# Ordering a hybrid decoder layer's instructions on the scheduler's timeline model instead of its plain one

## The chip, the cores and the metric

One core of a Trainium2 chip runs the kernel. The metric is the device time of one execution in microseconds (us); lower is better. The core's engines are TensorE (PE in the rows, with its weight loads as PEld), VectorE (DVE), ScalarE (ACT), GpSimd (POOL) and the queue of SyncE (SP), which issues every transfer of this kernel. Each of them executes its own list of instructions, one after the other, and waits on semaphores for the others. Which instruction stands where in these five lists is what this document is about.

## What is computed

The reference is one decoder layer on 1024 tokens of width 1024 in float32. Cut to what matters:

```
h = rms_norm(x, norm_mix); proj = h @ w_in            # q, k/v of three branches, gates, hq, hf, hi, hg
o_nsa  = gated sum of compressed, selected and window attention  (8 heads of 64, blocks of 128 queries)
o_hgrn = chunked gated linear recurrence, 4 heads of 128, then rms_norm and a silu gate
x = x + concat(o_nsa, o_hgrn) @ w_out
h = rms_norm(x, norm_ffn); gate, up = split(h @ w_gate_up)   # D_FF = 2816
x = x + (silu(gate) * up) @ w_down
```

## The kernel before

**Split products.** Large products are made of three matmuls each (`mm3`, lines 117 to 119), on a high and a low part of both operands. `split` (lines 110 and 111, with a gain 113 and 114) makes the parts: ScalarE writes the high part, VectorE subtracts it from the source for the low part. So nearly every block of weights passes ScalarE and then VectorE before TensorE can use it. The large projections also use a scheme with seven block products in place of eight, whose sums and differences are made on VectorE and GpSimd.

**The stages**, with the time at which each runs in the profile before: 

- Start (0 to 105 us): seven products of `product4` (called in lines 400 to 410) for two of the input projection's column groups. `acts5` to `acts7` and `acts3` build sums of the activations (lines 334, 349, 362, 381), `weights5` to `weights4` differences of the weights on GpSimd, `x_in` scales the input on GpSimd (line 288), `x_stats` squares the tokens on ScalarE (line 273), and `done1` to `done7` take the results out of PSUM. Products run one after the other on TensorE.
- Recurrence heads (about 105 to 280 us): `head` and `hgrn_head`. A head has seven levels, each with four small float32 matmuls (line 472, which the profile shows as eight), some VectorE work on them (lines 477 to 483), and then the next level. The projection of the next head (`dim_tile`, lines 117 to 119 on `hT_h`, `whi`) has no such chain and fills TensorE between the levels.
- Keys and values (about 280 to 410 us), then attention (410 to 750 us): a loop over units (query block, group, branch) with `score` (lines 918 to 929), `values` (940 to 945) and `prep` (854 to 892). The output projection and, near the end, first pieces of the feed-forward part are placed among the units by hand-set constants (`FILL`, `EXTRA`, `EARLY`, `NFIRST` and others).
- Change-over (750 to 800 us): `operand` (lines 803 to 807) transposes and splits the normalised activations, with sums on GpSimd (1066 to 1068). The last token block's norm is a chain of small VectorE instructions (`rsqrt`, lines 124 to 130) that ends in line 822.
- Gate and up projections (800 to about 1200 us): `gate_up_b` and its helpers, 22 rounds of seven products. Products to be used later go to DRAM (`act_store`, line 1120).
- Down projection (to the end): seven calls of `chain`. Weights come in pages of 512 KB into `rpage`, a ring of three buffers (line 1202); stored products come back in loads of up to 1 MB (line 1184); four 1 MB loads of the residual (`x_load`, line 1208) go to `res`. The third chain's weights (`weights5`, line 1256) are differences of two pages, made on GpSimd.

**What sets the order.** The kernel is written with a tile framework. Python code lists all instructions once, in the order in which it is written; the framework knows what each reads and writes and which buffer it needs. When the `TileContext` of lines 1355 and 1356 closes, its scheduler plays the program through on a model of the machine. Whenever an engine of the model is free, it takes, among the instructions whose inputs and buffers are ready in the model, the one that was written first. So an instruction overtakes one written earlier only where the earlier one is not ready in the model at that moment. The resulting lists are fixed when the program is built: on the chip each engine keeps to its list, and waits where the chip is not as far as the model was. In the program before, 1782 of 7092 instructions on TensorE and 819 of 1967 on VectorE stand ahead of one that was written earlier.

The model before is the framework's plain one: it gives an instruction a duration and an engine a time at which it is free.

## Time and profile before

| | us |
|---|---|
| median of 3 runs | 1424.68 (1423.24 to 1426.06) |
| time of the profiled execution | 1428.78 |
| its span, first to last instruction | 1426.9 |
| TensorE busy | 1371.6 (96%) |
| VectorE busy | 1096.2 (77%) |
| ScalarE busy | 617.7 (43%) |
| GpSimd busy | 444.7 (31%) |

Busy time is the time in which an engine had an instruction under way, so 1426.9 less 1371.6 is what TensorE stood still. The mean granted clock of TensorE was 0.99 of full speed. The profiled execution's time is 1.88 us more than its span.

### The profile page before, as it was taken

The page shows a single profiled execution, that of the slowest core. Times are in us where ns is not written, and L with a number is a line of the kernel's source. Part 1 is how long each engine was busy: PE and PEld are TensorE (multiplying, and loading weights), DVE is VectorE, ACT ScalarE, POOL GpSimd, SP SyncE. Part 2 cuts the span into 40 slices and gives each one's busy share as a digit, 9 for nine tenths or more (in the row PEclk, how much of TensorE's full clock was granted, in tenths as well). Part 3 has the DMA queues.
Part 4 walks back from the last instruction along what each step waited for, and adds up shares of the span by engine and source line. Part 5 has one row for each costly group of instructions (what it writes and reads, how often), then busy time and mean ns, then how long its engine had stood idle before and what let it go on. Part 6 is the DMA issues. An engine that isn't in the chain of part 4 may idle for free.

```text
span 1426.9 us, 20201 instructions
## 1 busy us (share of the span) xinstructions
PE 1371.6 (96%) x7224; PEld 1134.1 (79%) x7224; DVE 1096.2 (77%) x1967; ACT 617.7 (43%) x1203; POOL 444.7 (31%) x377
## 2 busy tenths in 40 slices
PE   8699999999999999999998999999999999999998
PEld 6578888999977777777776788888888888867877
DVE  8985888725778888888867888888888886547874
ACT  5652333333346656666665433333333333424332
POOL 8510111102034433344335432233233320028330
PEclk9899999999999999999999999999999999999999
DMA  7541110121130001000003223333333238976532
GB/s 280 193 118 45 31 30 9 34 71 43 45 134 1 1 1 59 31 16 30 17 15 104 90 94 106 110 97 111 111 111 111 90 110 310 315 244 220 178 115 93
DMA packets 112804, 139.94 MB, mean 98 GB/s; under 512 B 6304, under 2 KB 65856, under 8 KB 112704
## 3 DMA queue, kind: packets, MB, share of 16 engines
q1 hardware_dynamic: 112704, 138.66, 29.6%
q8 instruction: 57, 0.93, 0.3%
q14 instruction: 43, 0.35, 0.1%
HBM read 110.06 MB, written 28.57 MB: 97 GB/s over the span
## 4 chain that ended last, share of the span: by engine, by line
PE 73%; DVE 15%; issue 3%; DMA 3%; POOL 2%; ACT 2%; SPq 0%; ACTq 0%; POOLq 0%; DVEq 0%
PE bank L118 7%; PE bank L119 7%; PE a L118 7%; PE bank L117 7%; PE a L117 7%; PE a L119 7%; PE ps_t L117 4%; PE ps_t L119 4%; PE ps_t L118 4%; DVE wop L111 3%; PE ps_t L940 3%; PE a L944 2%; DMA rpage<-in_w_down_dram 2%; PE a L945 2%; PE ps_t L472 1%
## 5 line engine op out<-in xcount | busy, mean ns | idle before, releaser
L110 ACT ACTIVATE wop<-rpage 128x512 fp32r<-128x512 f32 x180 | 112.2, 626 | 155.7 <-PE bank L119 70.3
L929 POOL TENSOR_SCALAR pbig<-pbig,den,gates 128x640 f32<-128x640 f32 (+7 forms) x128 | 103.4, 811 | 165.7 <-DVE den L928 146.5
L111 DVE TENSOR_TENSOR wop<-rpage,wop 128x512 fp32r<-128x512 f32 x180 | 139.6, 779 | 5.2 <-ACT wop L110 3.1
L943 DVE TENSOR_TENSOR ph<-ps_t,ph 128x512 fp32r<-128x512 f32 x126 | 84.3, 683 | 17.8 <-ACT ph L942 17.0
L942 ACT ACTIVATE ph<-ps_t 128x512 fp32r<-128x512 f32 x126 | 72.6, 595 | 49.0 <-PE ps_t L940 38.4
L118 PE MATMUL bank<-wop 128*128 128x512 f32 x175 | 71.0, 407 | 11.3 <-DVE wop L111 11.3
L940 PE MATMUL ps_t<-ident,pbig 128*128 128x128 f32 x504 | 78.2, 274 | 2.1 <-POOL pbig L929 2.1
L1091 POOL TENSOR_TENSOR tmp<-tmp,rpage 128x512 f32<-128x512 f32 x21 | 31.2, 1486 | 138.6 <-DVE wop L111 130.8
L117 PE MATMUL bank<-wop 128*128 128x512 f32 x175 | 71.2, 408 | 3.2 <-ACT wop L110 2.3
L478 POOL TENSOR_TENSOR kp<-kp,fp 128x256 f32<-128x256 f32 x28 | 20.3, 724 | 162.3 <-PE bank L455 110.7
L119 PE MATMUL bank<-wop 128*128 128x512 f32 x175 | 70.0, 401 | 0.0
L940 PEld LDWEIGHTS ps_t<-ident,pbig 128*128 128x128 f32 x504 | 60.6, 140 | 11.5 <-POOL pbig L929 3.2
L111 DVE TENSOR_TENSOR wop<-act_a,wop 128x512 fp32r<-128x512 f32 x48 | 45.7, 953 | 29.5 <-ACT wop L110 29.4
L117 PE MATMUL a<-whi,hT_h 128*128 128x256 f32 (+1 forms) x232 | 66.6, 287 | 0.0
L118 PE MATMUL a<-wlo,hT_h 128*128 128x256 f32 (+1 forms) x232 | 66.4, 286 | 0.0
L119 PE MATMUL a<-whi,hT_l 128*128 128x256 f32 (+1 forms) x232 | 66.2, 285 | 0.0
L927 ACT ACTIVATE pbig<-ps_s,nm 128x640 f32<-128x640 f32 (+3 forms) x64 | 55.9, 874 | 23.6 <-DVE nm L926 18.2
L1051 POOL TENSOR_TENSOR tmp<-rpage 128x512 f32<-128x512 f32 x20 | 27.2, 1360 | 118.0 <-DMA rpage<-in_w_gate_up_dram 118.0
L110 ACT ACTIVATE wop<-act_a 128x512 fp32r<-128x512 f32 x48 | 30.2, 629 | 72.2 <-PE bank L119 53.2
L926 DVE TENSOR_REDUCE nm<-ps_s 128x1 f32<-128x640 f32 (+3 forms) x64 | 58.1, 914 | 4.2 <-PE ps_s L921 2.8
L944 PE MATMUL a<-ph,kv 128*128 128x512 f32 x132 | 58.6, 444 | 1.8 <-ACT ph L942 1.0
L945 PE MATMUL a<-ph,kv 128*128 128x512 f32 x132 | 56.9, 431 | 2.9 <-DVE ph L943 2.3
(485 smaller groups left out, 4460.1 us busy)
## 6 DMA issues: line engine op xcount, KB each, us to landing
rpage<-in_w_gate_up_dram SPq DMA_DIRECT2D x86, 256.0 KB, 3.1
rpage<-in_w_down_dram SPq DMA_DIRECT2D x40, 512.0 KB, 4.6
act_a<-act_d SPq DMA_DIRECT2D x12, 1024.0 KB, 7.6
act_d<-as SPq DMA_DIRECT2D x33, 256.0 KB, 2.2
rpage<-in_w_in_dram SPq DMA_DIRECT2D x14, 512.0 KB, 5.2
act_e<-act_d SPq DMA_DIRECT2D x6, 1024.0 KB, 7.9
act_d<-tmp SPq DMA_DIRECT2D x22, 256.0 KB, 2.1
act_d<-th SPq DMA_DIRECT2D x22, 256.0 KB, 2.1
```

What stands on the lines that cost most here:

```text
L110: A.activation(hi, src, AF.Copy)
L111: V.tensor_tensor(lo, src, hi.bitcast(F32), op=OP.subtract)
L117: PE.matmul(o, ah, bh, start=first, stop=False, skip_group_check=chained)
L118: PE.matmul(o, ah, bl, start=False, stop=False, skip_group_check=chained)
L119: PE.matmul(o, al, bh, start=False, stop=last, skip_group_check=chained)
L926: V.tensor_reduce(nm, sv, axis=AX.XY, op=OP.max, negate=True)
L929: G.tensor_scalar(pp, pp, den, gates[:, qb, h * 3 + 1 + b:h * 3 + 2 + b], op0=OP.mult, op1=OP.mult)
L940: PE.transpose(pt[:, r * P:(r + 1) * P], wts[r][:, c0:c0 + P], ident)
L942: A.activation(ph[:, 0], pt, AF.Copy)
L943: V.tensor_tensor(ph[:, 1], pt, ph[:, 0].bitcast(F32), op=OP.subtract)
L944: PE.matmul(o, vst[b][:, kb, g, :], ph[:, 0], start=b == 0 and kb == kb0, stop=False)
L945: PE.matmul(o, vst[b][:, kb, g, :], ph[:, 1], start=False, stop=False)
```

## The change

One argument of the `TileContext` is set, so that the scheduler plays the program on the framework's other model, in which each engine, each sequencer and each queue has a timeline of its own (an instruction's decoding, its wait, its execution and the landing of its result are separate pieces). No instruction of the kernel, no operand, no buffer and no constant is edited. What may differ in the program is the place of each instruction in its engine's list, the buffer of a ring that it gets, and the waits that follow from both.

```diff
-    with _tile.TileContext(nc) as tc:
+    with _tile.TileContext(nc, schedule_with_timeline_sim=True) as tc:
         hybrid_layer(tc, *args)
```

## Rows read from the trace of the kernel before

**Rows 1.** The page's first part: busy time, share of the span, instructions.
```profile
PE 1371.6 (96%) x7224; PEld 1134.1 (79%) x7224; DVE 1096.2 (77%) x1967; ACT 617.7 (43%) x1203; POOL 444.7 (31%) x377
```
**Rows 2.** Busy time of each engine by stage: stretch, length, then engines; clock, DMA.
```profile
0.00:100.00 100.00, 80.11 (x310) 62.79 (x311) 91.75 (x136) 58.80 (x100) 57.59 (x44) 0.93 0.59 195
100.00:400.00 300.00, 295.82 (x2050) 269.14 (x2049) 203.43 (x509) 102.30 (x212) 31.62 (x37) 1.00 0.16 46
400.00:700.00 300.00, 289.43 (x1709) 228.42 (x1707) 249.57 (x563) 187.24 (x429) 122.06 (x135) 0.99 0.08 30
700.00:800.00 100.00, 91.00 (x482) 69.93 (x482) 75.51 (x159) 56.54 (x108) 49.67 (x38) 0.98 0.18 53
800.00:1244.00 444.00, 444.00 (x1960) 367.80 (x1959) 357.83 (x466) 147.31 (x241) 116.81 (x80) 1.00 0.41 136
1244.00:1300.00 56.00, 50.13 (x195) 38.08 (x195) 25.78 (x35) 18.57 (x33) 19.31 (x15) 0.94 0.73 246
1300.00:1426.90 126.90, 121.14 (x527) 97.89 (x525) 92.34 (x104) 46.97 (x83) 47.69 (x30) 1.00 0.42 143
```
**Rows 3.** The same view, four stretches of 5 us in the start.
```profile
35.00:40.00 5.00, 1.84 (x6) 0.66 (x4) 5.00 (x8) 3.01 (x6) 5.00 (x5) 1.00 0.00 0
40.00:45.00 5.00, 2.02 (x4) 1.33 (x5) 5.00 (x8) 4.65 (x9) 1.60 (x2) 0.58 0.87 274
55.00:60.00 5.00, 1.09 (x5) 0.56 (x3) 5.00 (x7) 3.60 (x7) 1.97 (x2) 1.00 0.77 245
85.00:90.00 5.00, 1.94 (x6) 1.28 (x6) 5.00 (x10) 3.52 (x6) 0.00 (x0) 0.86 0.00 0
```
**Rows 4.** Timeline of VectorE in the start: start us, us, line, instruction.
```profile
52.33 1.79 DVE L111 TENSOR_TENSOR hT_l<-kv,hT_h 128x512 fp32r<-128x512 f32 x1
54.04 1.79 DVE L362 TENSOR_TENSOR qtok<-kv,sums 128x512 f32<-128x512 f32 x1
55.76 3.57 DVE L381 TENSOR_TENSOR qtok<-kv,sums 128x512 f32<-128x512 f32 x4
59.25 0.68 DVE L111 TENSOR_TENSOR wop<-sums,wop 128x512 fp32r<-128x512 f32 x1
```
**Rows 5.** Timeline of ScalarE just before.
```profile
51.10 0.63 ACT L110 ACTIVATE wop<-sums 128x512 fp32r<-128x512 f32 x1
```
**Rows 6.** Timeline of TensorE there; in brackets the idle time and its releaser.
```profile
60.58 0.50 PE L118 MATMUL bank<-wop 128*128 128x512 f32 x1 [4.50 <-DVE wop L111]
```
**Rows 7.** Line 111, 25 to 66 us: count, least, median and largest ns.
```profile
L111 DVE TENSOR_TENSOR wop<-sums,wop x8: 676/678/1775, 24.2 to 60.5; 128x512 fp32r<-128x512 f32 x8
L111 DVEq EVENT_SEMAPHORE  x6: 21/21/21, 27.2 to 54.9; - x6
```
**Rows 8.** Timelines of VectorE and TensorE in the change-over.
```profile
773.21 0.71 DVE L129 SCALAR_TENSOR_TENSOR rs_t<-rs_t,rs_v 128x1 f32<-128x1 f32 x1
773.44 0.52 PE L803 MATMUL bank<-ident,d 128*128 128x128 f32 x3 [0.72 <-DVE opA L807]
774.44 0.72 DVE L130 SCALAR_TENSOR_TENSOR n_rs<-rs_t,n_rs 128x1 f32<-128x1 f32 x1
775.69 2.31 DVE L822 SCALAR_TENSOR_TENSOR x<-x,n_rs,rpage 128x1024 f32<-128x1024 f32 x1
775.83 0.50 PE L119 MATMUL a<-opA,wop 128*128 128x512 f32 x1 [0.84 <-DVE wop L111]
```
**Rows 9.** The chain of waits in the third chain of the down projection.
```profile
1245.99 6.97 DMA rpage<-in_w_down_dram
1253.13 1.14 POOL tw_p L1256
...
1286.71 2.58 DMA rpage<-in_w_down_dram
```
**Rows 10.** Timeline of the transfer queue before that: issue time, time in the queue.
```profile
1225.17 0.50 SPq L1208 DMA_DIRECT2D res<-x_d  x1
1235.51 0.43 SPq L1208 DMA_DIRECT2D res<-x_d  x1
1240.97 0.94 SPq L1208 DMA_DIRECT2D res<-x_d  x1
```
**Rows 11.** Busy time of each engine over one recurrence head.
```profile
168.00:207.20 39.20, 38.40 (x232) 32.19 (x231) 34.07 (x87) 12.66 (x27) 5.01 (x7) 1.00 0.10 28
```
**Rows 12.** Timeline of TensorE in that head: one level's matmuls, one of the fill's.
```profile
177.01 1.15 PE L472 MATMUL ps_t<-qp,kv 128*128 128x128 f32 x8
177.91 0.48 PE L119 MATMUL a<-hT_h,wlo 128*128 128x512 f32 x1
...
180.13 1.16 PE L472 MATMUL ps_t<-qp,kv 128*128 128x128 f32 x8
```

## The prediction

> **What bounds the kernel now.** I read the page's busy times first, then busy time by stage, and then, where a stage leaves TensorE idle, the timelines of the engines in front of it. TensorE is busy for 1371.6 us [rows 1] of a span of 1426.9. The change neither adds nor takes away a matmul, so the whole stake in the faster direction is the 55.3 us in which TensorE stands still, and what its clock loses after such pauses. By stage [rows 2] that idle time is 19.9 us in the start, 4.2 from 100 to 400, 10.6 in the main part of attention, 9.0 around the change-over, none from 800 to 1244, 5.9 from 1244 to 1300 and 5.8 from there to the end. The sum is 55.3 again.
>
> These stages have different limits. In the start VectorE is full: 5.00 of 5 us in each of the four stretches in which TensorE has its longest pauses, with 1.84, 2.02, 1.09 and 1.94 us of matmuls [rows 3]. One pause can be followed to an instruction. TensorE waits 4.50 us for line 111 [rows 6], which starts at 59.25; its first input left ScalarE at 51.73 (51.10 and 0.63) [rows 5]. Between the two, VectorE ran line 111 for a later product, line 362 and four times line 381 [rows 4]. Line 381 prepares the product at line 409, while TensorE waited for the one at line 407. On the chip these stood in the wrong order, and that is what a closer model could mend. The recurrence heads are near the limit of two engines: of 39.2 us TensorE has 38.40 and VectorE 34.07 [rows 11]. From 800 to 1244 TensorE never stops, and its order there is the written one. Around 1250 the chain of waits is load, GpSimd difference, load: 6.97 us for the first page, 2.58 for the last [rows 9]. The ring of three pages holds the next load back there, not the order alone.
>
> **The change part by part.** It moves instructions and nothing else; I cost it stage by stage, against the profiled execution (span 1426.9, time 1428.78, which is 4.1 us or 0.3% above the median of 1424.68), and carry the difference to the median.
>
> Instructions added: none but waits. A wait of its own on VectorE takes 21 ns [rows 7]; a hundred more on one engine would be 2.1 us if none were covered. Their number may also fall, so I take 0, with 2.1 either way.
>
> Start: if the four line 381 instructions run behind the splits that TensorE waits for, 3.57 us [rows 4] leave a pause of 4.50 [rows 6]. VectorE is full, so the work moved back is in front of something else later; what is late next is the pause from 85 to 90 [rows 3]. I take half, -1.8. The bound below is the idle time of the first three stretches, 3.16 + 2.98 + 3.91 = -10.1. The bound above is the price of bad neighbours. The same instruction took 678 ns in the median and 1775 at most in this stretch [rows 7], when GpSimd was at work [rows 3]; all eight slow would be 8 x 1.10 = +8.8.
>
> The Trainium skill (SBUF — State Buffer, section Who interferes with whom) says that a VectorE instruction with two SBUF inputs and a GpSimd instruction that reads SBUF exclude each other for the whole instruction, whichever comes second. The row's two durations agree with it; by that rule a new order changes durations too, and the start could come out at the +8.8 in place of -1.8.
>
> Heads and keys, 100 to 400: 4.2 us idle in 300, TensorE fed by the fill. I take 0; a gain of 4.2 is the bound below, and the first rival is the bound above.
>
> Attention, 400 to 700: 10.6 us idle in 300 against 4.2 in the 300 before [rows 2]. VectorE (249.57) and ScalarE (187.24) both have room, so the excess of 6.4 is order and latency. I take a quarter, -1.6; the bounds are that excess won or doubled, 6.4 either way.
>
> Change-over, 700 to 800: two small norm instructions (0.71 and 0.72 us) stand between the splits for which TensorE waits 0.72 and 0.84 us [rows 8], and line 822 takes 2.31 us of VectorE right behind. Put after the splits, the two give back -1.4; the bounds are half of the stage's 9.0 idle us, 4.5 either way. The chain they belong to ends the last token block, so it can't be put off far.
>
> Gate and up, 800 to 1244: no idle time, written order, every buffer ring in its turn: 0. What hides a shift of VectorE or of the stores there is TensorE's own 444 us; VectorE has 86 us to spare. If VectorE were given its splits so late that the 86 us were used up, each us beyond them would be one of the total; nothing in the rows points that way.
>
> Down projection: 195 matmuls in 56 us, against 4.41 a us before [rows 2], are 52 too few, or 11.8 us. SyncE's queue issues three 1 MB residual loads (line 1208) just ahead of the slow pages [rows 10]. They are ready whenever the queue has nothing else to do, in either model, so I take 0. If they went elsewhere, half of the 11.8 could be won, and if more large loads came in front, as much lost: 5.9 either way. The queue is one list: what it is moved past counts here, and a page behind one 1 MB load more is late by that load.
>
> Sum: -1.8 - 1.6 - 1.4 = -4.8 us. Span 1422.1, profiled 1424.0, median 1419.9; I forecast **1420**.
>
> **The rivals.** *A critical matmul behind the fill* (slower). The fixed lists hold each level's eight matmuls of a recurrence head between fill matmuls [rows 12]. If the new model takes fill earlier, VectorE gets each level later. The head has 39.2 - 34.07 = 5.1 us of VectorE room, over seven levels 0.73 us each; from that point on TensorE runs out of fill before the chain ends. The levels in the row are 3.1 us apart. Five more fill matmuls in front, at 0.23 (444 us by 1960, [rows 2]), are 1.1 us a level: 7.9 - 5.1 = 2.8 a head, 11.2 over four heads, so 1424.7 + 11.2 = 1435.9. For it: both engines are close to full there and the order before leaves only 0.8 us a head. Against it: a model closer to the chip should see the chain too.
>
> *Neighbours on VectorE and GpSimd* (slower): the start's splits on VectorE meet GpSimd's sums and differences more often, +8.8 [rows 7], 1433.5. It decides where TensorE has no matmul in hand, as in the four stretches of [rows 3]. This is the rule of the Trainium skill (SBUF — State Buffer, Who interferes with whom) that was weighed above.
>
> *The order hardly matters* (no change): pauses are set by the ring of pages, by VectorE's total in the start (91.75 of 100 us, [rows 2]) and by the first load, and TensorE's work is fixed. Then 1424.7. That the new model gives the old lists, so that the change does nothing, belongs here too; with 819 of 1967 VectorE instructions out of written order already, I give that little.
>
> *The whole of the start and of the pages* (faster by more): -10.1 and -5.9, 1408.7.
>
> **How the numbers follow.** About 0.2%, 2.9 us, is what a measurement of this kernel can tell from no change. The forecast gets 0.34 (its own range 1412 to 1422), the large gain 0.12, no change 0.18, the fill rival 0.28 and the neighbours 0.08. So faster 0.46, same 0.18, slower 0.36. Cases of both signs hold most of the chance, so the range is wide. Down it reaches the large gain with the change-over's bound, 1408.7 - 4.5 = 1404. Up it takes the fill rival's 1435.9 and most of the start's bound of 8.8 with it, 1444.
>
> **What would show it.** Right: line 381 behind line 407's splits on VectorE and the pause of 4.5 us near 58 below 2; from 400 to 700 TensorE idle under 9 us; around 775 the norm's small instructions behind the splits; the same matmuls, a busy time of TensorE near 1371 and no idle time from 800 to 1240. Fill rival: heads further apart than 39.2 us, with VectorE waiting for line 472. Neighbours: line 111 in the start at a median near 1.7 us. I am wrong if a stage that I set to 0 moves most, above all the 444 us of the gate and up products or the pages of the down projection.

## The result, and the profile after

The changed kernel takes 1482.01 us (four runs, 1479.4 to 1485.77) for 1425.2 of the kernel before: a ratio of 1.0403, with a 95% interval from 1.0373 to 1.0432. The prediction was 1420, range 1404 to 1444. It had the wrong sign and the wrong size.

The work is the same: the page's busy times, next to [rows 1], show the same instruction counts, TensorE busy 6.4 us longer and VectorE 18.6.

```profile
PE 1378.0 (93%) x7224; PEld 1148.2 (78%) x7224; DVE 1114.8 (75%) x1967; ACT 618.9 (42%) x1203; POOL 455.1 (31%) x377
```

Next, busy time by stage, as [rows 2], but cut at the borders of the work. The borders are read from TensorE's timeline: the first matmul of line 455 (first recurrence head), the last of line 526, the first of line 940 (attention), the last of line 958, the last of line 803, the first of the down projection. In the tables and below, the stages between these borders are called start, heads, keys, attention, change-over, gate/up and down.

```profile
0.00:130.10 130.10, 110.85 (x447) 88.64 (x448) 106.16 (x153) 68.51 (x114) 57.81 (x44) 0.93 0.52 167
130.10:349.00 218.90, 193.53 (x1300) 179.01 (x1300) 142.16 (x334) 62.47 (x122) 28.02 (x28) 0.95 0.10 27
349.00:445.90 96.90, 95.24 (x721) 90.56 (x720) 65.55 (x194) 33.95 (x88) 16.54 (x14) 1.00 0.28 94
445.90:808.30 362.40, 328.15 (x1893) 257.13 (x1893) 278.62 (x623) 216.79 (x481) 138.28 (x148) 1.00 0.05 18
808.30:846.60 38.30, 27.44 (x147) 22.04 (x147) 32.93 (x51) 19.19 (x36) 24.57 (x17) 0.82 0.37 101
846.60:1255.90 409.30, 409.30 (x1800) 338.73 (x1800) 341.62 (x433) 132.84 (x216) 122.41 (x82) 1.00 0.34 111
1255.90:1477.60 221.70, 213.51 (x925) 172.05 (x923) 147.74 (x182) 85.15 (x148) 67.45 (x44) 1.00 0.62 213
```

The heads and the keys of the kernel before, in the same way:

```profile
128.70:281.70 153.00, 149.49 (x968) 129.50 (x967) 131.53 (x331) 52.39 (x105) 20.26 (x28) 1.00 0.10 28
281.70:416.60 134.90, 132.58 (x1040) 128.14 (x1039) 74.27 (x194) 45.03 (x106) 15.60 (x12) 1.00 0.25 81
```

All stages at the same borders in the kernel before, and in the runs that follow (us; each line adds up to the span of the run's profiled execution, 1426.9 before and 1477.6 after):

| run | start | heads | keys | attention | change-over | gate/up | down |
|---|---|---|---|---|---|---|---|
| before | 128.7 | 153.0 | 134.9 | 335.4 | 35.9 | 409.7 | 229.3 |
| after | 130.1 | 218.9 | 96.9 | 362.4 | 38.3 | 409.3 | 221.7 |
| e1_heads_back | 128.8 | 178.2 | 135.4 | 360.6 | 38.7 | 408.7 | 222.2 |
| e2_heads_forth | 129.4 | 209.9 | 102.3 | 335.1 | 36.2 | 408.1 | 225.4 |
| e3_pe_back | 133.7 | 179.8 | 134.6 | 352.7 | 39.3 | 408.9 | 223.9 |
| e4_fill_256 | 130.2 | 213.2 | 96.8 | 361.7 | 38.3 | 409.5 | 223.1 |
| e5_pe_dve_back | 132.2 | 153.1 | 136.0 | 346.7 | 35.6 | 408.3 | 229.1 |
| e6_four_back | 130.4 | 153.1 | 134.9 | 335.5 | 35.9 | 408.1 | 224.1 |
| e7_dve_forth | 140.1 | 179.9 | 134.3 | 356.6 | 40.2 | 408.7 | 227.2 |
| e8_down_forth | 128.4 | 153.0 | 134.9 | 335.5 | 35.9 | 409.7 | 221.9 |
| e9_copy_first | 128.8 | 164.8 | 134.9 | 334.3 | 35.9 | 409.7 | 226.0 |
| e10_fill_first | 128.0 | 166.5 | 134.9 | 336.4 | 35.9 | 408.1 | 226.8 |
| e11_act_forth | 134.3 | 153.2 | 136.0 | 347.2 | 36.2 | 408.4 | 224.9 |
| e12_sum_back | 139.9 | 173.7 | 134.3 | 359.6 | 40.2 | 408.5 | 223.4 |
| e13_fold_first | 130.7 | 153.2 | 134.9 | 335.3 | 35.9 | 408.1 | 227.4 |
| e14_attn_forth | 130.8 | 153.0 | 140.3 | 392.7 | 34.8 | 409.9 | 225.8 |
| e15_end_back | 140.2 | 162.1 | 134.3 | 356.7 | 39.7 | 408.6 | 223.4 |

The heads take 65.9 us more and the keys behind them 38.0 less, because fill (independent projection matmuls) that belonged to the keys' time was done in the heads; together they lose 27.9. Of this, 21.3 is time in which TensorE stands still (27.0 now, 5.8 before, by the rows above). The other 6.7 is longer busy time, with 13 more matmuls in the two stages and a mean granted clock of 0.95 in the heads, 1.00 before. The attention loses 27.0. The down projection shows 7.6 less, the rest moves by 3 at most.

TensorE's waits over the whole program (waiter, what came last; us in total, times, longest) name the places; before, these four were 0.6, 2.3, 2.4 and 3.7 us. The fifth line is VectorE's wait in the heads, 4.1 us before.

```profile
PE bank L526 <- DVE qp L523: 13.2, 2, 6.6
PE a L945 <- DVE ph L943: 11.6, 23, 1.7
PE ps_t L472 <- DVE qp L477: 10.2, 9, 1.5
PE ps_s L918 <- ACT pbig L927: 6.1, 15, 0.7
DVE qp L477 <- PE ps_t L472: 22.0, 13, 3.4
```

TensorE's timeline in the first head, next to [rows 12], shows how a head looks now:

```profile
162.88 1.05 PE L472 MATMUL ps_t<-qp,kv 128*128 128x128 f32 x8
166.73 1.05 PE L472 MATMUL ps_t<-qp,kv 128*128 128x128 f32 x8
168.72 1.13 PE L472 MATMUL ps_t<-qp,kv 128*128 128x128 f32 x8 [0.94 <-DVE qp L477]
171.14 1.13 PE L472 MATMUL ps_t<-qp,kv 128*128 128x128 f32 x8 [1.29 <-DVE qp L477]
...
186.28 1.11 PE L526 MATMUL bank<-ident,qp 128*128 128x128 f32 x4 [6.61 <-DVE qp L523]
```

The early levels stand more than 6 us apart (143.98, 150.14, 156.30, 162.88), full of fill. The last ones are bare, with no fill between them: TensorE waits for VectorE, and then for 6.61 us at the head's end, where VectorE normalises the head and nothing is left to do beside it. The program's own list says the same. These are the fill matmuls behind each group of the chain's matmuls (two of line 455, then the seven levels of line 472; a dash is none):

```
              L455 L455  1   2   3   4   5   6   7   ahead of L526
before, head 1  12   9   4   9   6   5   7   7   -   2 + 34
before, head 2  13   9   4   9   6   5   7   7   -   2 + 34
after,  head 1  25  28  23  23  25  13   -   -   -   -
after,  head 2   -  29  25  24  18   -   -   -   -   -
```

Head 2 has 96 fill matmuls in both. In the old list they are dealt out so that each level has about what VectorE's chain needs, and 34 cover the head's end. In the new list all 96 are gone after the third level. Only the first three heads run bare: the fourth has fill behind every level, the fill of the keys. VectorE's list has changed too. In all 28 levels both masked copies L483 now stand ahead of the sum L480, in none before.

Over the whole program 2900 of 6948 matmuls now stand ahead of one written earlier, 1638 before (the figure of 1782 of 7092 given further up counts all of TensorE's instructions, not its matmuls alone); on VectorE 1045 of 1967, 819 before.

### The profile page after: what moved, and what is told of

Read it like the earlier page. It is cut to its first block, busy times and chain, and to the rows that moved or that the text cites. A ratio compares the mean times of both kernels' runs of the same rounds, so it can differ in the third digit from the quotient of the medians.

```text
span 1477.6 us, 20109 instructions
## 1 busy us (share of the span) xinstructions
PE 1378.0 (93%) x7224; PEld 1148.2 (78%) x7224; DVE 1114.8 (75%) x1967; ACT 618.9 (42%) x1203; POOL 455.1 (31%) x377
## 4 chain that ended last, share of the span: by engine, by line
PE 74%; DVE 14%; DMA 4%; issue 3%; POOL 3%; ACT 2%; SPq 0%; ACTq 0%; POOLq 0%; DVEq 0%
PE a L119 9%; PE a L117 9%; PE a L118 9%; PE bank L118 7%; PE bank L119 7%; PE bank L117 7%; PE ps_t L117 4%; PE ps_t L119 4%; PE ps_t L118 4%; DVE wop L111 2%; DVE nm L926 2%; DMA rpage<-in_w_down_dram 2%; DVE ph L943 2%; PE ps_t L940 2%; PE a L945 2%
## 5 line engine op out<-in xcount | busy, mean ns | idle before, releaser
L111 DVE TENSOR_TENSOR wop<-rpage,wop 128x512 fp32r<-128x512 f32 x180 | 145.9, 813 | 16.4 <-ACT wop L110 14.4
L478 POOL TENSOR_TENSOR kp<-kp,fp 128x256 f32<-128x256 f32 x28 | 28.0, 1001 | 210.8 <-PE bank L455 110.8
L118 PE MATMUL bank<-wop 128*128 128x512 f32 x175 | 70.0, 400 | 5.3 <-DVE wop L111 5.2
L945 PE MATMUL a<-ph,kv 128*128 128x512 f32 x132 | 60.1, 455 | 13.1 <-DVE ph L943 11.6
L119 PE MATMUL bank<-wop 128*128 128x512 f32 x175 | 69.1, 395 | 0.0
L117 PE MATMUL bank<-wop 128*128 128x512 f32 x175 | 64.7, 401 | 1.9 <-ACT wop L110 1.9
L111 DVE TENSOR_TENSOR wop<-tmp,wop 128x512 fp32r<-128x512 f32 x42 | 44.6, 1063 | 18.8 <-ACT wop L110 18.0
```

The costliest lines, as they stand in the source:

```text
L111: V.tensor_tensor(lo, src, hi.bitcast(F32), op=OP.subtract)
L117: PE.matmul(o, ah, bh, start=first, stop=False, skip_group_check=chained)
L118: PE.matmul(o, ah, bl, start=False, stop=False, skip_group_check=chained)
L119: PE.matmul(o, al, bh, start=False, stop=last, skip_group_check=chained)
L945: PE.matmul(o, vst[b][:, kb, g, :], ph[:, 1], start=False, stop=False)
```

## The experiments

**How lists were exchanged.** Both schedulers emit the same instructions in the same five lists (one per engine, and SyncE's transfers), in different order. So one engine's list, or a stretch of it, can be taken from the other program. Each instruction of the list gets an order-only dependency on the one ahead of it; the scheduler then orders only what is left free. So the lists that aren't pinned can change as well, and a run shows the pinned list together with what the scheduler arranges around it.

```diff
+def _pin(nc, tc, engine, text):
...
+    for a, b in zip(seq, seq[1:]):
+        tc.add_manual_dep(own[b], own[a].name, NOSYNC, reason="pin")
...
         hybrid_layer(tc, *args)
+        _pin(nc, tc, PE, ORDER_OF_BEFORE)
```

The long names in capitals stand for lists of instruction numbers, `PE` and the like for engines, `NOSYNC` for the order-only kind of dependency. e6_four_back shows below that the pins themselves cost nothing.

**TensorE's list of the heads, put back into the changed kernel (e1) and taken into the kernel before (e2).**

```diff
+        _pin(nc, tc, PE, HEADS_OF_BEFORE)   # e1, with the timeline
+        _pin(nc, tc, PE, HEADS_OF_AFTER)    # e2, without it
```

> The timeline model schedules everything, but TensorE's list for the four recurrence heads is pinned to the one of the kernel before (1064 matmuls). Theory A (the loss of the heads is TensorE's fill, taken in batches too long for the chain of a head): the heads are 39 us apart again instead of 51 to 58, and the time falls by the 29 us by which the first attention transpose (line 940) was late, to about 1453 (1445 to 1460). Theory B (the loss sits in the lists of the other engines, as in line 478 on GpSimd, whose mean rose from 724 to 1001 ns): the heads stay over 45 us apart and the time over 1470.

> The reverse: the plain model schedules everything, but TensorE's list for the four heads is pinned to that of the changed kernel. Theory A: the heads are 50 to 58 us apart and the time rises by about 29 us, to 1454 (1445 to 1462), though the lists of all other engines come from the plain model. Theory B: the heads stay near 40 us apart and the time within 10 us of 1425.

Measured: e1 1479.57 us, ratio 1.0379 (1.0344 to 1.0413); e2 1452.14, ratio 1.0182 (1.0161 to 1.0203). The second is what the fill theory said, the first is not. TensorE's new list of the heads costs 24.3 us net in the old program (heads +56.9, keys -32.6 in the table), most of the 27.9 of the changed kernel. The plain scheduler arranged the other lists around it: VectorE's heads changed too, but no level has both copies ahead of the sum. The bare levels show the difference: the last two of the first head are 2.08 us apart in e2, as shown here, and 2.42 in the changed kernel's fence (168.72 and 171.14):

```profile
167.98 1.13 PE L472 MATMUL ps_t<-qp,kv 128*128 128x128 f32 x8 [0.94 <-DVE fp L480]
170.06 1.13 PE L472 MATMUL ps_t<-qp,kv 128*128 128x128 f32 x8 [0.94 <-DVE fp L480]
```

But putting the old list back into the new program gives almost nothing back: the heads still take 178.2 us. Something else in the new program holds them then.

**TensorE's whole list put back (e3), and the fill in half-size matmuls (e4).**

```diff
+        _pin(nc, tc, PE, ORDER_OF_BEFORE)   # e3, with the timeline
```
```diff
-            sl = slice(hf * 512, (hf + 1) * 512)
-            for c in range(NK):
-                wh, wl = parts[c]
+            for q in range(2):
+                sl = slice(hf * 512 + q * 256, hf * 512 + (q + 1) * 256)
+                for c in range(NK):
...
```

> The timeline model schedules everything, but TensorE's whole list is that of the kernel before; the other four lists are free to differ. Theory A, carried to attention as well: nearly all of the loss is in TensorE's list, so the time is 1417 to 1430; if the 8 us that the changed kernel wins in the down projection come from the other lists, it is below 1425. Theory B: over 1450.

> The timeline model, and the heads' projections (dim_tile) as matmuls of 256 columns, twice as many and each half as long; no arithmetic is left out. In the changed kernel a batch of 23 to 28 fill matmuls of 512 columns, over 5 us, stands between two levels of a head. Theory A1 (the model hands TensorE a number of instructions ahead, whatever they take): still some 28 a batch, so half the time, 3.3 to 3.6 us, and the heads move closer, under 50 us apart; time 1460 to 1475. Theory A2 (the model reckons a level's work on VectorE as over 5 us long, and fills that time): some 50 a batch, the heads as far apart as in the changed kernel (51 to 58 us), time 1475 to 1490.

Measured: e3 1474.39 us, ratio 1.0331 (1.0312 to 1.035); e4 1474.71, ratio 1.0341 (1.0321 to 1.0362). In e3 TensorE does its matmuls in exactly the old order, and heads (179.8) and attention (352.7) are slow all the same: a list can be late on an engine that isn't the busiest. In e4 the list has 51, 37 and then mostly 28 halves behind a group, where the changed kernel has 25, 28 and 23 wholes. In head 1 that is 264 halves up to the last level, for 137 wholes; they reach further down the levels, but at the head's end none are left again. The batch of 28 and the time are what the first expectation said, but the heads stay 48.5 to 56.9 us apart, nearer to the second. They take 213 us for 219. Smaller pieces don't cure it.

VectorE's list in e3 shows what is late. It isn't the changed kernel's list, as the new model made it around TensorE's old one: 24 of its 28 levels have both copies ahead of the sum. The first fence is one level of a head in the kernel before, the second one in e3 (VectorE's and GpSimd's timelines).

```profile
184.49 0.76 DVE L477 TENSOR_TENSOR qp<-qp,fp 128x256 f32<-128x256 f32 x2
185.16 0.27 DVE L480 TENSOR_TENSOR fp<-fp 128x64 f32<-128x64 f32 x1
185.34 0.76 DVE L483 COPY_PREDICATED kv<-hm,ps_t 128x256 f32<-128x256 uint8 x2
185.57 0.64 POOL L478 TENSOR_TENSOR kp<-kp,fp 128x256 f32<-128x256 f32 x1 [1.29 <-DVE fp L480]
186.00 0.50 DVE L478 TENSOR_TENSOR kp<-kp,fp 128x256 f32<-128x256 f32 x1
```
```profile
197.91 0.75 DVE L483 COPY_PREDICATED kv<-hm,ps_t 128x256 f32<-128x256 uint8 x2
198.57 0.25 DVE L480 TENSOR_TENSOR fp<-fp 128x64 f32<-128x64 f32 x1
198.93 0.43 DVE L478 TENSOR_TENSOR kp<-kp,fp 128x256 f32<-128x256 f32 x1
198.97 0.90 POOL L478 TENSOR_TENSOR kp<-kp,fp 128x256 f32<-128x256 f32 x1 [1.60 <-DVE fp L480]
199.29 1.18 DVE L477 TENSOR_TENSOR qp<-qp,fp 128x256 f32<-128x256 f32 x2
```

Before, the sum L480, on which both halves of L478 wait, goes first, and the two masked copies L483 fill the time in which GpSimd does its half of L478. In e3 the copies go first, and GpSimd's half runs beside L478 and L477 on VectorE: 0.90 us for 0.64, and L477 takes 1.18 us for two instead of 0.76.

**Which engine's list: VectorE's as well put back (e5), then ScalarE's and GpSimd's too (e6), and e3's VectorE list taken forth (e7).**

```diff
+        _pin(nc, tc, PE, ORDER_OF_BEFORE)
+        _pin(nc, tc, DVE, ORDER_OF_BEFORE)   # e5, e6: with the timeline; e7: DVE's list of e3, without it
+        _pin(nc, tc, ACT, ORDER_OF_BEFORE)   # e6
+        _pin(nc, tc, POOL, ORDER_OF_BEFORE)  # e6
```

> The scheduler with the timeline, with TensorE's and VectorE's whole lists taken from the kernel before; ScalarE's, GpSimd's and the queues' lists stay the new ones. Theory B (VectorE's own list carries what was left after TensorE's list was put back: in each level of a head the masked copy L483 now stands ahead of the sum L480, on which the next level waits, and L478 and L477 on VectorE run beside L478 on GpSimd): 1425 to 1436 us, heads 39 to 40 us apart, L477 back from 549 ns to 420 ns in the mean. Theory C (ScalarE's, GpSimd's or the queues' lists carry it): above 1450 us, heads 44 us apart or more.

> The scheduler with the timeline, with the lists of TensorE, VectorE, ScalarE and GpSimd all taken from the kernel before: what is left of the change is SP's queue alone. If the queue's order carries nothing: 1426 us within 3. If the gain of some 6 us that the changed kernel shows in the down projection is the queue's (its fetches issued in another order): 1418 to 1422 us. If the queue carries a loss: above 1432 us.

> The plain scheduler with TensorE's list of before, and VectorE's list of the run e3_pe_back. Theory B (VectorE's list alone makes the loss of e3_pe_back): 1455 to 1475 us, heads 44 to 48 us apart, attention (first to last matmul of L940 to L958) 345 to 355 us for 335 before. Theory C (ScalarE, GpSimd or the queues): below 1435 us.

Measured: e5 1442.59 us, ratio 1.0113 (1.0097 to 1.013); e6 1426.24, ratio 1.0002 (0.9991 to 1.0013); e7 1485.74, ratio 1.0421 (1.0402 to 1.044). e5 brings the heads back to 39.2 us apart and leaves 11 us in the attention and some 4 in the start, so it lies between the two theories: of the loss of e3, VectorE's list carries the heads, and ScalarE's or GpSimd's a part of the rest. e6 is the kernel before again: SyncE's new order is worth nothing either way. e7 is above its 1455 to 1475. TensorE's list is as before, and e3's VectorE list with what follows from it costs as much as the whole change: 27 us in the heads, 21 in the attention, 11 in the start. What follows includes ScalarE's list, which differs from that of before in 258 of 1203 places, 151 of them in the attention, so the 21 us there aren't shown to be VectorE's alone.

**The down projection alone (e8).**

```diff
+        _pin(nc, tc, PE, DOWN_OF_AFTER)   # and DVE, ACT, POOL, SP; without the timeline
```

> The plain scheduler with the lists of all five engines taken from the changed kernel in the down projection alone (the last 924 matmuls, SP's last 100 fetches). If the 6 to 7 us that the changed kernel wins behind the gate and up products are its order there: 1417 to 1421 us, faster than both kernels. If they come from the state that the earlier stages leave (what has been fetched by then): 1424 to 1428 us.

Measured: 1422.12 us (12 runs), ratio 0.9977 (0.9968 to 0.9986), the fastest of all kernels here. That is between the two expectations. The gain is real but half as large as the profiles say: 3.4 us by the medians for 7.4 in the stage (229.3 to 221.9). The stage takes 224.1 us in e6 and 227.4 in e13, with the old order in it on all four compute engines; the profiled execution of the kernel before was a long one (1428.78 us for a median of 1425.2). In e8, ScalarE and GpSimd run their instructions in the same order of lines and tiles as before, so the gain comes from TensorE's or VectorE's order there, with SyncE's or without. In the stage's row of e8 TensorE is idle for 8.8 us, 11.6 before.

```profile
1197.40:1419.30 221.90, 213.08 (x925) 172.15 (x923) 148.39 (x182) 85.27 (x148) 67.44 (x44) 1.00 0.63 213
```

**One place at a time, in the kernel before: the copies ahead of the sum (e9), the fill ahead of the chain (e10), ScalarE's list (e11).** The edits are changes of a list. In e9 `477 477 480 483 483 478` becomes `477 477 483 483 480 478` in all 28 levels. In e10 the fill behind the levels 1 to 7 of the first three heads, `4 9 6 5 7 7 -`, becomes `13 12 13 - - - -` (the 19 behind levels 4 to 6 move; the expectation says 21), and that of the fourth head likewise.

```diff
+        _pin(nc, tc, PE, ORDER_OF_BEFORE)      # e10: FILL_FIRST instead, no other pin
+        _pin(nc, tc, DVE, COPY_FIRST)          # e9
+        _pin(nc, tc, DVE, ORDER_OF_BEFORE)     # e11, POOL too
+        _pin(nc, tc, ACT, ORDER_OF_E5)         # e11
```

> The plain scheduler with TensorE's list of before and VectorE's list of before but for one thing: in each of the 28 levels of the heads the sum L480 stands behind the masked copies L483 that followed it. Theory B (this place alone makes the heads' loss of the runs e3_pe_back and e7_dve_forth): two copies of 0.76 us each level ahead of what the next level waits for, 28 x 0.76 = 21 us, to 27 us with L477 slowed by GpSimd's L478 beside it: 1444 to 1454 us, heads 44 to 46 us apart, attention 335 us. Rival (the fill's work on VectorE between the levels, L546 to L556 and L111, makes it): below 1432 us, heads under 41 us apart.

> The plain scheduler with TensorE's list of before but for one thing: in each head the fill matmuls that stood behind the levels 4 to 7 (21 of 38 in the first three heads, most of them) are spread over levels 1 to 3, in the same order, so that levels 4 to 7 stand bare; no work is moved from one head to another or out of the heads. Theory A (fill costs nothing only while VectorE's chain of the same level runs): the moved fill, 0.23 us each, lengthens the early levels and the bare ones don't get shorter than VectorE's 2.4 us: some 3 to 6 us a head, 12 to 24 in all: 1437 to 1450 us, heads 42 to 45 us apart. Rival (TensorE is busy 97% of the heads, so the order of the same work is worth nothing): 1424 to 1429 us, heads 39 us apart.

> The plain scheduler with the lists of TensorE, VectorE and GpSimd of before, and ScalarE's list of the run e5_pe_dve_back. If ScalarE's order makes the 17 us of that run: 1438 to 1446 us, attention 344 to 350 us for 335 before. If GpSimd's order or the queue's makes it: below 1430 us, attention 335 to 337 us.

Measured: e9 1439.34 us, ratio 1.0101 (1.0081 to 1.012), heads 42 us apart; e10 1438.21, ratio 1.0095 (1.0075 to 1.0116), heads 41.5 to 43.8; e11 1442.39, ratio 1.0117 (1.01 to 1.0133), attention 347.2.

e9 falls between its two expectations. The place costs 11.8 us over 28 levels, 0.42 each and not 0.76 (what covers the rest was not traced); it is a cause, but less than half of VectorE's 27. The groups of the heads show the slowed pair: VectorE's L477 and GpSimd's L478 in e9, 420 and 724 ns in the mean before.

```profile
L477 DVE TENSOR_TENSOR qp<-qp,fp 128x256 f32<-128x256 f32 x56 | 27.1, 524 | 4.6 <-PE ps_t L472 4.0
L478 POOL TENSOR_TENSOR kp<-kp,fp 128x256 f32<-128x256 f32 x28 | 26.2, 937 | 168.1 <-PE bank L455 110.1 <-DVE fp L480 58.0
```

e10 bears the fill theory out: no matmul left its head, only 19 of them (some 4.3 us at 0.23) moved a few levels up, and the first two heads grew by 2.3 and 2.4 us, the third by 4.7, the fourth by 4.0. Of the 13.5 us, 9.2 are idle time of TensorE and 4.3 longer busy time, at a mean granted clock of 0.96 in the heads. VectorE's list wasn't pinned: the fill's L546 and L548 moved up with their matmuls in the first three heads, and no level has both copies ahead of the sum. The bare levels are 2.07 us apart, so the chain alone sets a pace, and TensorE stands still in it:

```profile
190.33 1.13 PE L472 MATMUL ps_t<-qp,kv 128*128 128x128 f32 x8 [1.18 <-DVE qp L477]
192.40 1.13 PE L472 MATMUL ps_t<-qp,kv 128*128 128x128 f32 x8 [0.94 <-DVE fp L480]
```

e11 answers what e5 left: with the lists of TensorE, VectorE and GpSimd as before, ScalarE's list alone gives e5's time and nearly its stages (17 us by the medians, 12 of them in the attention). In the start, TensorE waits 14.5 us for splits of line 110, 7.7 before.

**The rest of VectorE's loss in the heads: the sum put back into e7 (e12), a second thing put back (e15), and the fill's VectorE work one place earlier in the kernel before (e13).**

```diff
-... 477 477 483 483 480 478 ...
+... 477 477 480 483 483 478 ...           (e12: 18 of 28 levels of e7's list)
-... 516 ... 111 ... 552 ... 518 111 521 521 554 523 523
+... 516 ... 518 521 521 523 523 111 552 111 554   (e15: e12's list, end of head 3; head 2's alike; one 111 in head 1's)
-... 478 546 477 ...
+... 546 478 477 ...                       (e13: 12 places of the list of before)
```

> The kernel of e7_dve_forth (TensorE's list of before, VectorE's list as the model of e3_pe_back orders it) with one thing put back: in 18 of the 28 levels, where the copies L483 stand right ahead of the sum L480, the sum goes back in front of them. If the place of the sum costs as much here as in e9_copy_first (12 us for 28 levels): heads 42 to 43 us apart and 1473 to 1480 us. If the places add up to more together (a level delayed in two places misses TensorE's fill as well): heads back to 40 us, 1465 us or below. If the sum's place was no cause here: heads 44 to 48 us apart, 1483 us or more.

> VectorE's list of before but for one thing: the 12 places in the first three heads where a query or gate operation of the fill (L546 or L548, 0.68 us) stands right behind the chain's product L478 are swapped, the fill's operation first. Theory B2 (VectorE's 0.68 us of fill ahead of the chain lengthens a level like the copies do): 4 x 0.4 to 0.68 us a head, 5 to 8 us: 1430 to 1434 us, heads 40.8 to 42 us apart. Rival (the level has room, or the swap is hidden beside GpSimd's half of L478): within 2 us of 1425.5, heads 39.2 us apart.

> The kernel of e12_sum_back with a second thing put back on VectorE: at the end of the first three heads the fill's operations that stand among the head's normalisation ahead of L523 (three weight splits L111 of 1.21 us in the first two heads' ends and one more in the third, the second L552 and L554) go behind L523, where the kernel before has them. If they make TensorE's waits at L526 (10.8 us in e12_sum_back, 0.6 before): those waits under 3 us, heads 43 us apart in the mean, 1466 to 1471 us. If L523 is late for another reason (the head's chain itself ends late): waits at L526 stay over 7 us and the time within 3 us of 1476.7.

Measured: e12 1476.73 us, ratio 1.0357 (1.0332 to 1.0381); e13 1425.29, ratio 0.9996 (0.9987 to 1.0006); e15 1468.71, ratio 1.031 (1.0288 to 1.0333). e13 is a clean miss for its theory: a fill operation of 0.68 us ahead of VectorE's half of L478 costs nothing, in 12 places. Not every operation ahead of the chain counts. e12 wins 6.2 us in the heads (179.9 to 173.7), the size that it should. In e12 the trace shows where to look next, TensorE's waits in the heads:

```profile
PE bank L526 <- DVE qp L523: 10.8, 4, 4.2
PE ps_t L472 <- ACT kv L468: 6.2, 4, 1.6
```

and VectorE's timeline ahead of one of them, where two weight splits of the fill (the second starts at 224.77), L552 and L554 stand among the head's last operations, ahead of L523:

```profile
220.91 1.22 DVE L111 TENSOR_TENSOR wlo<-wraw,whi 128x1024 fp32r<-128x1024 f32 x1 [0.32 <-ACT whi L110]
222.76 0.69 DVE L552 TENSOR_TENSOR fp<-a,kv 128x512 f32<-128x512 f32 x1
224.77 1.21 DVE L111 TENSOR_TENSOR wlo<-wraw,whi 128x1024 fp32r<-128x1024 f32 x1
225.90 0.42 DVE L554 TENSOR_SCALAR kp<-fp 128x512 f32<-128x512 f32 x1
226.24 1.28 DVE L523 TENSOR_TENSOR qp<-qp,gmix 128x512 f32<-128x512 f32 x2
226.97 0.66 PE L526 MATMUL bank<-ident,qp 128*128 128x128 f32 x4 [4.25 <-DVE qp L523]
```

e15 moves nine such operations behind L523, and the heads fall by 11.6 us more, to 162.1, with the wait nearly gone:

```profile
PE bank L526 <- DVE qp L523: 2.3, 4, 0.7
```

So of the 26.9 us that VectorE's list costs in the heads of e7, the sum's place is 6.2, the ends of the heads 11.6; 9.1 are left, of which 6.2 is the wait of L472 for ScalarE above: once a head, at the third level, behind the one place where the list still has the copies (in the first three heads L548 too) ahead of the chain's products. That place wasn't tried by itself. How far this carries over to the changed kernel differs: its own VectorE list has the copies ahead of the sum in every level, but between L516 and L523 it has nothing but the head's own operations, in all four heads. The 11.6 us belong to e3's list; in the changed kernel the head's end waits because the fill is gone.

**TensorE's list in the attention alone (e14).**

```diff
+        _pin(nc, tc, PE, ATTENTION_OF_AFTER)   # without the timeline
```

> The plain scheduler with TensorE's list of the changed kernel in the attention alone (the other engines' lists are the plain scheduler's own). If TensorE's order carries its own part of the attention's 27 us (362 in the changed kernel against 353 with TensorE's list back): attention 343 to 350 us, 1434 to 1441 us. If the attention's loss is only VectorE's and ScalarE's: 334 to 338 us, 1424 to 1428 us.

Measured: 1489.4 us, ratio 1.0441 (1.0416 to 1.0466); the attention takes 392.7 us, far more than in the changed kernel. TensorE's waits there name the place: its new list takes the output projection early, and the pages for it (lines 606, 607) come late.

```profile
PE a L117 <- DVE rpage L606: 17.7, 4, 11.9
PE a L119 <- DVE rpage L607: 10.8, 6, 2.9
```

The other lists aren't those of before either: the plain scheduler arranged them around this one, and VectorE's has 12 of the 16 conversions of line 606 in the first third of the operations of line 943, as the changed kernel has, for 8 before. So this run can't size TensorE's part, nor is it shown why the pages are late. What the exchanges do show is that parts of them don't add up. In heads and keys, TensorE's new heads list in the old program costs 24, e3's VectorE list beside TensorE's old one 26, and the changed kernel with all its own lists 28.

## Why the prediction was wrong

- **Heads and keys.** This is the step that failed. It was set to 0 with the fill rival as its upper bound of 11.2; it is +27.9. The rival named the mechanism and a sign for it (heads further apart than 39.2, VectorE waiting for line 472), and both came: 51.3 to 57.9 us, and 22.0 us of waits for 4.1. But it was priced by five more fill matmuls a level, evenly. In the first two heads the program after has 12 to 21 more behind each group from the second of line 455 to the third level and none behind the last ones, and the price is the cover, the fill beside the chain, that the late levels and the head's end lose. e2 shows it at 24.3 us. [Rows 11] said how little room there was (0.8 us of 39.2 on TensorE); the reading should have asked what happens to a stage that lives on even dealing once the dealing changes, and priced the bare end: from the start of L516 to the end of L523 7.7 us of VectorE's time pass in a head of the kernel before (198.75 to 206.45), and 34 fill matmuls, 7.8 us at 0.23, were kept for them. The copies ahead of the sum on VectorE weren't among the cases at all. e9 shows that they cost 11.8 us by themselves in the old program, and the changed kernel has them in every level; the 3.6 us between e2's 24.3 and 27.9 fit its longer bare levels, but weren't tried there by themselves.
- **Attention.** This step failed too: -1.6 was taken, 6.4 either way; it is +27.0. The argument was that VectorE and ScalarE "both have room", which is an average. e7 and e11 show 21 and 12 us of loss there with TensorE's list as before, e11 by ScalarE's list alone, in engines that are busy 274 and 215 of 335 us. In VectorE's list of the changed kernel 12 of the 16 page conversions of line 606, which the output projection needs, stand in the first third of the 132 operations of line 943, 8 of 16 before: output projection early, attention late. That resembles the heads, but e7 loses its 21 us with 8 of 16, so it isn't shown to be the cause. Which places make the loss stays open.
- **Start.** -1.8 with the pause near 58 us as its reason. The place was right: that pause is 2.06 us now for the 4.50 of [rows 6], and line 381 is dealt out among the splits. The stage gained nothing from it (130.1 for 128.7): up to 130 us TensorE's waits for VectorE's line 111 fell from 12.2 to 7.6 us, but those for ScalarE's line 110 rose from 7.7 to 11.6. The neighbours rival isn't seen at the size that was set for it: line 111 has the same median, 678 ns, as in [rows 7]. But from 25 to 66 us five of its instructions take over 1.7 us, three before.
- **Change-over.** -1.4, bounds 4.5 either way; it is +2.4. Around 830 the norm's small instructions of lines 129 and 130 still stand between two splits, so the move that was counted on did not come.
- **Gate and up.** 0, and it is -0.4, with TensorE never idle: right.
- **Down projection.** 0 with 5.9 either way; the profiles say -7.6, the medians of e8 -3.4. By the medians the bound held, by the profiles it did not; the gain exists. That it is the queue's is not so: with SyncE's new list alone (e6) nothing is won, so the place asked about, the residual loads of [rows 10], is not what pays. Whether TensorE's order or VectorE's pays in e8 stays open.
- **The chances.** "A model closer to the chip should see the chain too" was the argument against the rival that came true. It spoke of what the model should do; the rows spoke of how little there was to win (55.3 us idle, 4.2 of them from 100 to 400) and how tight the balance was.

## What to carry to other kernels

Where an engine is nearly always busy (38.40 of 39.2 us in a head here) because independent work is dealt out evenly beside a chain, the order is the asset: a list that takes this work early spends the cover early and leaves the chain bare later. Price a re-ordering by the cover that each stage would lose (how long is the chain with nothing beside it), not by the idle time that it could win. And an exchange of lists, engine by engine and stage by stage, finds the place quickly. But look at the lists that weren't exchanged, too, as the scheduler may have changed them. The parts don't add up, and the stage that gained can be kept alone, as in e8_down_forth (1422.12 us, faster than both kernels).

## What the runs showed of the hardware

An order can change durations. GpSimd's half of L478 took 0.64 us beside VectorE's masked copies, which read PSUM and a mask, and 0.90 us beside VectorE's L478 and L477, and L477 took 1.18 us for two there and 0.76 in the level of the kernel before. The Trainium skill (SBUF — State Buffer, Who interferes with whom) says that a VectorE instruction with two SBUF inputs and a GpSimd instruction that reads SBUF contend for a port pair that one holds for its whole duration; the trace agrees in these places. In the start, where the prediction had weighed the rule, both programs have line 111 at 678 ns in the median and at over 1.7 us at most.
